# Matmuls of a product ordered by width, a first pair of accumulators in other PSUM banks, and two small moves at a phase change

## The chip, the core and the metric

The kernel runs on one core of one Trainium2 chip. The metric is the device time of an execution in microseconds (us). Engines are named as in the profile: PE is TensorE (matmuls), DVE is VectorE, ACT is ScalarE, POOL is GpSimd, SP is SyncE, which here only issues transfers (DMAs).

## What is computed

One encoder layer on 512 tokens of width 2048 in float32, and a last RMS norm. With `conv` a depthwise convolution over the tokens, and `attend` a neighbourhood attention on an 8 x 64 grid of tokens with 16 heads of 64:

```python
xn = rms_norm(x, attn_norm_g)
u_val, u_gate, q, k, v = split(xn @ w_in)            # 2048 -> 5 x 1024
a = silu(layer_norm(conv(u_val * sigmoid(u_gate), 31 taps)))
b = attend(q, k, v, rpb)
x = x + concat(rms_norm(a), rms_norm(b)) @ w_out     # 2048 -> 2048
up = conv(rms_norm(x) @ w_up, 3 taps)                # 2048 -> 2 x 5632
gate, val = split(up)
x = x + (silu(gate) * val) @ w_down                  # 5632 -> 2048
out = rms_norm(x, final_norm_g)
```

## The kernel before, in words

**Precision.** Each float32 weight tile is loaded as `raw` (128 x 1024, 512 KB) and split into two tiles of a reduced format (float32r): ACT copies the high half `whi` (L125), and DVE subtracts it from the raw tile for the low half `wlo` (L126). The other operands are split in the same way. A full product takes three matmuls: high by high, low by high, high by low (`mm3`, L138, L141, L142).

**Weights.** `plan` is a list of all weight units in order of use. `weights()` hands out the next one and makes the loads and splits of the units up to three further on (AHEAD = 3). Four tiles of `whi` and of `wlo` exist (NW = 4), and nine of `raw`.

**Order.** The tile framework's scheduler orders each engine's queue by priorities, which follow the program text; `shifted(by)` changes them for a block, and `pin` keeps an instruction in program order. Side work (statistics, factors, residual loads) is written as generators: `steps` is a list of them, and `tick(m)`, called behind a matmul, runs one more step of the first one, with its instructions issued after that matmul. PSUM has eight banks: three under the tag "mm", two under "sc" (one tile of two banks), two under "tr" and one under "po".

**Stages.** (times of the profiled execution)

1. To about 505 us: projection and attention. `first_glu` (L337) does the first two output tiles together, in two "mm" banks; then `project` (L315 on) does one tile of 48 matmuls after the other, each in an "mm" bank. `gated` (L350 on) takes a pair of tiles: DVE multiplies the gate tile by `rstd` (L352), ACT takes the sigmoid (L353), DVE multiplies twice more (L354, L356, the latter reads the second tile and writes `ch`), and 31 steps of the convolution follow on DVE (L363, L367). `stats1` computes `rstd`, which needs a square root on ACT (L225), two matmuls of `ones` (`st`, L237) and a copy (L239). Ahead of all that, a tiny activation (L109) runs on ACT, with the function Copy.
2. To about 703 us: the output projection.
3. 703 to 1578 us, the up stage. For each of 44 f's, `up` (L685 on) computes two tiles (gate and value) by seven products of half the size (a Strassen-Winograd scheme; products in the order TURN = 3, 2, 4, 5, 1, 0, 6). In six of the products the operand is one tile of 512 columns, high half and low half beside each other (256 each): for each of 8 blocks of the weight one matmul of the high weight by all 512 columns (L694), and one of the low weight by the 256 high columns (L697), in turn. Product 2 uses `mm3` with 256 columns. Accumulators `pa`, `pd_`, `pb`, `pe`, `pc_` are copied between products: ACT copies `pa` into `pd_` (L704) before product 4 may add to `pa`. Sums of weights are made on DVE (L653, L655) and by accumulating DMAs. Afterwards `hidden` multiplies by a norm factor (L748, L749), convolves (`conv3`: ACT L737, DVE L738, L739) and multiplies gate and value; results go to DRAM.
4. From 1578 us: the down stage. Seven products again (TURN2 = 3, 0, 4, 1, 2, 6, 5), each of 22 units of weight; a unit has 12 matmuls of 512 columns on four accumulators (L819, L820, L821). The left operands `ho` are made by `operand` (ACT L776 for the high half, DVE L777 for the low one) from the hidden tiles, which are read back from DRAM except for the last four. `again` makes operands ahead, into the list `pre`, while the last f runs: one operand, of hidden tiles that are not written to DRAM. `four` gives the accumulators: for products 3, 4, 2 and 5 two in the "sc" banks, where `pa` lay, and two in the "tr" banks; for products 0, 1 and 6 three "mm" banks and the "po" bank. `factors3` (L850 on) loads four tiles of the final norm's weights (`g3`) and multiplies two of them by -1 (L855); it is put into `steps` ahead of product 3. `taken` and `ready` add residual and accumulators; `write` normalises and stores at the end.

Of the kernel before, what the change touches and what calls it, by code (L numbers as in the profile page):

```python
# [10 lines left out]
F32 = mybir.dt.float32  # L11
F32R = mybir.dt.float32r
AF = mybir.ActivationFunctionType
ALU = mybir.AluOpType
AX = mybir.AxisListType

P = 128
D = 2048
S = 512
# [15 lines left out]
U = 8  # L35
# [5 lines left out]
H = S // 2  # L41
NK = NF // 2
KEEP = 4
# [10 lines left out]
TURN2 = (3, 0, 4, 1, 2, 6, 5)  # L54
Q = D // 2 // S
# [17 lines left out]
def layer(ctx: ExitStack, tc: tile.TileContext, xT, xn, w_in, w_out, w_up, w_down, par, tab, g3, out):  # L73
    nc = tc.nc
# [5 lines left out]
    psm = ctx.enter_context(tc.tile_pool(name="psm", bufs=3, space=bass.MemoryType.PSUM))  # L80
    psa = ctx.enter_context(tc.tile_pool(name="psa", bufs=1, space=bass.MemoryType.PSUM))
# [9 lines left out]
    def t2(name, dt=F32):  # L91
        return tp.tile([P, S], dt, tag="t2k", name=name)
# [13 lines left out]
    ones = consts.tile([P, P], F32, name="ones")  # L106
    nc.vector.memset(ones, 1.0)
    idle = t2("idle")
    nc.scalar.activation(idle[:, :1], ones[:, :1], AF.Copy)  # L109
    ps = psm.tile([P, S], F32, tag="mm", name="warm")  # L110
    for _ in range(WARM):
        nc.tensor.matmul(ps[:, :P], ones, ones, start=True, stop=True)
# [5 lines left out]
    def raw_unit(src, n):  # L118
        raw = t4([P, U * P], "raw")
        return raw, nc.sync.dma_start(raw[:, :n], src)  # L120

    def parts(raw, n):
        hi = wpool.tile([P, U * P], F32R, tag="whi", name="whi", bufs=NW)
        lo = wpool.tile([P, U * P], F32R, tag="wlo", name="wlo", bufs=NW)
        i = nc.scalar.activation(hi[:, :n], raw[:, :n], AF.Copy)  # L125
        j = nc.vector.tensor_sub(lo[:, :n], raw[:, :n], hi[:, :n].bitcast(F32))  # L126
        return hi, lo, i, j
# [5 lines left out]
    tight = []  # L133
# [11 lines left out]
    steps, asteps = [], []  # L145
# [105 lines left out]
    pin = tc.keep_in_program_order  # L251
# [24 lines left out]
    for j, n in enumerate((NC_, 0)):  # L276
        raw, i = raw_unit(w_in[n, :, U * P:2 * U * P], U * P)
        pin(i)
        w = parts(raw, U * P)
# [9 lines left out]
    for step in ORDER:  # L289
        i = next(a_ if step == "a" else q_)  # L290
# [44 lines left out]
        late.append(lambda: gated(i, pg, pv))  # L335

    def first_glu():  # L337
        two = [psm.tile([P, S], F32, tag="mm", name="pj") for _ in range(2)]
        for u in range(KD // U):
            ws = weights(), weights()  # L340
            for k in range(U):
                kk = u * U + k
                for ps, w in zip(two, ws):
                    hi, lo, at = w[k]
                    m = mm3(ps, (hi, lo), at, xs[kk][0], xs[kk][1], kk == 0, kk == KD - 1)
            for _ in range(2):
                tick(m)
        late.append(lambda: gated(0, *two))
# [180 lines left out]
    p, n = -1, 0  # L529
# [51 lines left out]
    comb = [[] for _ in range(7)]  # L581
# [85 lines left out]
    order2 = [*range(NK - KEEP // 2, NK), *range(NK - KEEP // 2)]  # L667
# [17 lines left out]
    def up(f, done):  # L685

        def product(c, ps, more):
            hi, lo = wt = weights()
            for k in range(U):
                m, w = comb[c][k], slice(k * P, (k + 1) * P)  # L690
                if c == 2:
                    i = mm3(ps[:, :H], wt, k, m[:, :H], m[:, H:], k == 0, k == U - 1)
                    continue
                i = nc.tensor.matmul(ps, hi[:, w], m, start=k == 0 and not more, stop=False, skip_group_check=more)  # L694
                if k == 0 and tight:
                    pin(i)
                i = nc.tensor.matmul(ps[:, :H], lo[:, w], m[:, :H], start=False, stop=k == U - 1,  # L697
                                     skip_group_check=more)
            tick(i)
            done(TURN.index(c), i)  # L700

        def copied(to, ps):
            with shifted(-100):
                nc.scalar.activation(to, ps, AF.Copy)  # L704

        def folded(to, ps):
            nc.scalar.activation(to, ps[..., H:], AF.Copy)
            add(to, to, ps[..., :H])

        product(3, pa, False)  # L710
        tight[:] = [1] * (f > 0)
        copied(pd_, pa)
        product(2, pc_, False)
        w = t2("w")[:, :H]
        nc.scalar.activation(w, pc_[:, :H], AF.Copy)
        product(4, pa, True)
        copied(pe, pa)
        product(5, pd_, True)
        g = t2("g")
        folded(g[:, :H], pd_)  # L720
        product(1, pa, True)
        copied(pb, pa)
        product(0, pe, True)
        v = t2("vl")
        by = v.rearrange("p (i t) -> p i t", i=2)
        folded(by[:, 1], pa)
        folded(by[:, 0], pe)
        add(by, by, w.unsqueeze(1).broadcast_to([P, 2, H]))
        product(6, pb, True)
        folded(g[:, H:], pb)  # L730
        return g, v
# [26 lines left out]
    def operand(c, k):  # L758

        if c in (3, 5, 6):  # L760
            src = hs[2 * k + (c != 3)][:, H if c == 6 else 0:][:, :H]
        else:
            (b11, b12), (b21, b22) = ((hs[i][:, :H], hs[i][:, H:]) for i in (2 * k, 2 * k + 1))
            t = t2("hc")
            src, m = t[:, :H], t[:, H:]
            if c == 2:
                nc.vector.tensor_sub(src, b22, b12)
            elif c == 1:
                nc.vector.tensor_sub(src, b11, b12)
            else:  # L770
                nc.vector.tensor_sub(m, b11, b12)
                nc.vector.scalar_tensor_tensor(src, b22, -1.0, m, op0=ALU.mult, op1=ALU.subtract)
                if c == 0:
                    nc.vector.scalar_tensor_tensor(src, src, -1.0, b21, op0=ALU.mult, op1=ALU.subtract)
        t = t2("ho", F32R)
        nc.scalar.activation(t[:, :H], src, AF.Copy)  # L776
        nc.vector.tensor_sub(t[:, H:], src, t[:, :H].bitcast(F32))  # L777
        return t
# [3 lines left out]
    pre = []  # L782

    def again(at, i):
        if at == 1:
            pre.extend(operand(TURN2[0], k) for k in order2[:KEEP // 2 - 1])
        for _ in range(6):
            if back:
                f = back.pop(0)
                hs[f] = t2("h")  # L790
                behind(nc.gpsimd.dma_start(hs[f], hd[f]), i)
# [56 lines left out]
    gs = []  # L848

    def factors3():  # L850
        for d in range(2 * Q):
            g = t2("g3")
            nc.sync.dma_start(g, g3[:, d * S:(d + 1) * S])
            if d >= Q:
                nc.vector.tensor_scalar(g, g, -1.0, None, op0=ALU.mult)  # L855
            gs.append(g)
            yield

    sq = [sm.tile([P, 2, 2 * Q], F32, tag="sq", name="sq") for _ in range(2)]
# [1 line left out]
    def taken(x, ps):  # L861

        for a, b in zip(x, ps):
            add(a, a, b)
            yield
# [36 lines left out]
    def run(c, ps, more):  # L902
        for _ in product2(c, ps, more):
            pass
# [3 lines left out]
            yield from x  # L908

    a = four(True)  # L910
    steps.append(factors3())
    run(3, a, False)
    e3 = rest(0, 0)
    steps.append(taken(e3, a))
    b = four(False)
    run(0, b, False)
    e0 = rest(0, 1)
    steps.append(taken(e0, b))
    run(4, a, True)
    e4 = rest(1, 0)  # L920
    steps.append(taken(e4, a))
    b = four(False)
# [78 lines left out]
```

## Time and profile before

| | us |
|---|---|
| median of 3 runs | 2015.14 (2013.87 to 2018.29) |
| the profiled execution's own time | 2016.07 |
| its span in the trace | 2014.3 |
| mean granted clock of PE | 0.997 |
| PE busy | 1994.4 |
| DVE busy | 1599.6 |
| ACT busy | 1105.2 |

A row of the timeline has start and duration in us, engine, line of the kernel, operation, tiles (written <- read), shape and count, and in brackets the idle time before it with the instruction or transfer that ended it. Matmuls overlap in the rows, since the next one starts before the one ahead has left the array; the distance between starts is the time that one costs. In the table of windows a row has the stretch, its length, and the busy time of each engine with its count of instructions, then the clock that PE was granted (1.00 is full), the share of the DMA engines' time, and GB/s.

### The profile page before, as it was taken

What the parts mean: (1) busy time and instruction counts of PE and PEld (TensorE: products, weight loads), DVE (VectorE), ACT (ScalarE), POOL (GpSimd) and SP (SyncE); (2) the same over time, 40 slices, a digit from 0 to 9 for tenths busy, and PEclk for the clock granted to TensorE, in tenths of its full rate; (3) what the DMA queues carried; (4) which work ended last, traced back from release to release, by engine and by line L of the source; (5) the groups of instructions that cost most, each with busy time, mean ns of one, the idle gap of its engine ahead of it and who ended that gap; (6) DMA issues with size and microseconds to landing.
All of it is one profiled execution on the core that took longest, in us unless ns stands there. A gap on an engine that the chain in (4) does not pass through costs nothing.

```text
span 2014.3 us, 28373 instructions
## 1 busy us (share of the span) xinstructions
PE 1994.4 (99%) x10525; PEld 1685.5 (84%) x10525; DVE 1599.6 (79%) x2296; ACT 1105.2 (55%) x1729; POOL 226.1 (11%) x310
## 2 busy tenths in 40 slices
PE   9999999999999999999999999999999999999998
PEld 7878888877788888888888888888888788888886
DVE  5994798498547888888888888888888798886765
ACT  7234423448525676666666666666666645554654
POOL 0110111110001111111111111111110400000000
PEclk9999999999999999999999999999999999999999
DMA  9677767776858879998999999999986976666563
GB/s 341 167 218 181 177 170 202 183 182 199 256 147 220 203 206 263 244 267 235 265 240 258 253 253 251 251 256 248 258 239 170 375 229 212 218 212 195 191 210 114
DMA packets 143114, 451.01 MB, mean 224 GB/s; under 512 B 15232, under 2 KB 23936, under 8 KB 141568
## 3 DMA queue, kind: packets, MB, share of 16 engines
q1 hardware_dynamic: 90608, 293.98, 43.6%
q0 software_dynamic: 42624, 148.92, 34.2%
q10 hardware_dynamic: 9744, 6.30, 1.0%
q8 instruction: 82, 1.34, 0.3%
q14 instruction: 56, 0.46, 0.1%
HBM read 430.27 MB, written 111.15 MB: 269 GB/s over the span
## 4 chain that ended last, share of the span: by engine, by line
PE 94%; DMA 2%; DVE 2%; ACT 1%; issue 0%; SPq 0%; DVEq 0%; ACTq 0%
PE pu L694 25%; PE pu L697 12%; PE pd L821 7%; PE pd L819 7%; PE pd L820 7%; PE pj L138 6%; PE pj L141 6%; PE pj L142 6%; PE po L138 3%; PE po L141 3%; PE po L142 3%; PE pu L141 2%; PE pu L138 2%; PE pu L142 2%; DVE y L367 1%; DMA xn<-in_xn 1%
## 5 line engine op out<-in xcount | busy, mean ns | idle before, releaser
L125 ACT ACTIVATE whi<-raw 128x1024 fp32r<-128x1024 f32 x572 | 605.5, 1059 | 722.4 <-PE pj L141 211.7
L126 DVE TENSOR_TENSOR wlo<-raw,whi 128x1024 fp32r<-128x1024 f32 x572 | 699.0, 1223 | 304.1 <-ACT whi L125 274.9
L694 PE MATMUL pu<-xc,whi 128*128 128x512 f32 x2112 | 748.2, 399 | 0.0
L697 PE MATMUL pu<-xc,wlo 128*128 128x256 f32 x2112 | 593.1, 281 | 0.0
L694 PEld LDWEIGHTS pu<-xc,whi 128*128 128x128 f32 x2112 | 396.8, 188 | 96.9 <-issue 0.2
L697 PEld LDWEIGHTS pu<-xc,wlo 128*128 128x128 f32 x2112 | 399.0, 189 | 0.3 <-issue 0.2
L138 PE MATMUL pj<-xh,whi 128*128 128x512 f32 x624 | 246.8, 398 | 1.4 <-DVE gate L352 1.4
L142 PE MATMUL pj<-xh,wlo 128*128 128x512 f32 x624 | 243.7, 390 | 0.8 <-DVE wlo L126 0.8
L141 PE MATMUL pj<-xl,whi 128*128 128x512 f32 x624 | 244.4, 392 | 0.1
L821 PE MATMUL pd<-whi,ho 128*128 128x512 f32 x616 | 240.1, 391 | 4.0 <-DVE ho L777 4.0
L819 PE MATMUL pd<-whi,ho 128*128 128x512 f32 x616 | 240.5, 391 | 0.5 <-ACT ho L776 0.5
L820 PE MATMUL pd<-wlo,ho 128*128 128x512 f32 x616 | 240.4, 390 | 0.0
L367 DVE SCALAR_TENSOR_TENSOR y<-ch,prm,y 128x507 f32<-128x507 f32 (+14 forms) x240 | 169.9, 742 | 3.2
L194 POOL DMA_DIRECT2D ws<-in_w_down x88 | 79.4, 902 | 568.1 <-DMA ws<-ws 279.0
L138 PEld LDWEIGHTS pj<-xh,whi 128*128 128x128 f32 x624 | 117.5, 188 | 30.2 <-issue 3.5
L821 PEld LDWEIGHTS pd<-whi,ho 128*128 128x128 f32 x616 | 116.0, 188 | 29.3 <-DVE ho L777 5.3
L142 PEld LDWEIGHTS pj<-xh,wlo 128*128 128x128 f32 x624 | 117.5, 188 | 26.1 <-DVE wlo L126 1.3
L141 PEld LDWEIGHTS pj<-xl,whi 128*128 128x128 f32 x624 | 117.7, 189 | 24.0 <-DVE xl L257 0.5
L819 PEld LDWEIGHTS pd<-whi,ho 128*128 128x128 f32 x616 | 115.9, 188 | 25.1 <-ACT ho L776 0.9
L820 PEld LDWEIGHTS pd<-wlo,ho 128*128 128x128 f32 x616 | 116.1, 188 | 24.6 <-DVE wlo L126 0.3
L643 POOL DMA_DIRECT2D raw<-in_w_up x88 | 85.2, 968 | 344.6 <-DMA raw<-in_w_up 85.6
L138 PE MATMUL pu<-xc,whi 128*128 128x256 f32 x352 | 99.7, 283 | 0.5 <-ACT xc L586 0.5
(185 smaller groups left out, 2524.4 us busy)
## 6 DMA issues: line engine op xcount, KB each, us to landing
raw<-in_w_up SPq DMA_DIRECT2D x220, 512.0 KB, 8.0
ws<-in_w_down POOLq DMA_DIRECT2D x132, 512.0 KB, 7.7
raw<-in_w_up POOLq DMA_DIRECT2D x88, 512.0 KB, 9.8
raw<-ws SPq DMA_DIRECT2D x88, 512.0 KB, 4.3
raw<-in_w_in SPq DMA_DIRECT2D x78, 512.0 KB, 5.1
raw<-in_w_down SPq DMA_DIRECT2D x66, 512.0 KB, 4.2
ws<-ws POOLq DMA_DIRECT2D x44, 512.0 KB, 7.9
raw<-in_w_out SPq DMA_DIRECT2D x32, 512.0 KB, 5.1
```

What stands on the lines that cost most here:

```text
L125: i = nc.scalar.activation(hi[:, :n], raw[:, :n], AF.Copy)
L126: j = nc.vector.tensor_sub(lo[:, :n], raw[:, :n], hi[:, :n].bitcast(F32))
L138: i = nc.tensor.matmul(ps, hi[:, a], mh, start=start, stop=False, skip_group_check=more)
L141: nc.tensor.matmul(ps, hi[:, a], ml, start=False, stop=False, skip_group_check=more)
L142: return nc.tensor.matmul(ps, lo[:, a], mh, start=False, stop=stop, skip_group_check=more)
L367: nc.vector.scalar_tensor_tensor(y[:, a:b], h[:, a + j - PAD:b + j - PAD], prm[:, o + j:o + j + 1], y[:, a:b], op0=ALU.mult, op1=ALU.add)
L643: nc.gpsimd.dma_start(a[c], w_up[f, q2], accum_op=ALU.add)
L694: i = nc.tensor.matmul(ps, hi[:, w], m, start=k == 0 and not more, stop=False, skip_group_check=more)
L697: i = nc.tensor.matmul(ps[:, :H], lo[:, w], m[:, :H], start=False, stop=k == U - 1, skip_group_check=more)
L819: nc.tensor.matmul(ps[i], h[:, t], wh[:, d], start=start and not more, stop=False, skip_group_check=more)
L820: nc.tensor.matmul(ps[i], h[:, t], wl[:, d], start=False, stop=False, skip_group_check=more)
L821: return nc.tensor.matmul(ps[i], h[:, tl], wh[:, d], start=False, stop=stop, skip_group_check=more)
```

## The change

Four edits. In six of the seven products of an f, the eight matmuls with high weights and 512 columns come first, then the eight with low weights and 256 columns. The tiny first activation is a square root, and the two tiles of `first_glu` lie in the "tr" banks. `factors3` issues its four loads one per step and the two multiplications after all of them, and stands behind `taken(e0, b)`, which puts it into the third product (4) of the down stage. `again` makes two operands.

```diff
-    nc.scalar.activation(idle[:, :1], ones[:, :1], AF.Copy)
+    nc.scalar.activation(idle[:, :1], ones[:, :1], AF.Sqrt)
...
     def first_glu():
-        two = [psm.tile([P, S], F32, tag="mm", name="pj") for _ in range(2)]
+        two = [psa.tile([P, S], F32, tag="tr", name="pj", bufs=2) for _ in range(2)]
...
         def product(c, ps, more):
             hi, lo = wt = weights()
-            for k in range(U):
-                m, w = comb[c][k], slice(k * P, (k + 1) * P)
-                if c == 2:
+            if c == 2:
+                for k in range(U):
+                    m = comb[c][k]
                     i = mm3(ps[:, :H], wt, k, m[:, :H], m[:, H:], k == 0, k == U - 1)
-                    continue
-                i = nc.tensor.matmul(ps, hi[:, w], m, start=k == 0 and not more, stop=False, skip_group_check=more)
-                if k == 0 and tight:
-                    pin(i)
-                i = nc.tensor.matmul(ps[:, :H], lo[:, w], m[:, :H], start=False, stop=k == U - 1,
-                                     skip_group_check=more)
+            else:
+                for part, n in ((hi, S), (lo, H)):
+                    for k in range(U):
+                        i = nc.tensor.matmul(ps[:, :n], part[:, k * P:(k + 1) * P], comb[c][k][:, :n],
+                                             start=part is hi and k == 0 and not more,
+                                             stop=part is lo and k == U - 1, skip_group_check=more)
+                        if part is hi and k == 0 and tight:
+                            pin(i)
             tick(i)
             done(TURN.index(c), i)
...
         if at == 1:
-            pre.extend(operand(TURN2[0], k) for k in order2[:KEEP // 2 - 1])
+            pre.extend(operand(TURN2[0], k) for k in order2[:KEEP // 2])
...
     def factors3():
         for d in range(2 * Q):
-            g = t2("g3")
-            nc.sync.dma_start(g, g3[:, d * S:(d + 1) * S])
-            if d >= Q:
-                nc.vector.tensor_scalar(g, g, -1.0, None, op0=ALU.mult)
-            gs.append(g)
+            gs.append(t2("g3"))
+            nc.sync.dma_start(gs[d], g3[:, d * S:(d + 1) * S])
+            yield
+        for g in gs[Q:]:
+            nc.vector.tensor_scalar(g, g, -1.0, None, op0=ALU.mult)
             yield
...
     a = four(True)
-    steps.append(factors3())
     run(3, a, False)
     e3 = rest(0, 0)
     steps.append(taken(e3, a))
     b = four(False)
     run(0, b, False)
     e0 = rest(0, 1)
-    steps.append(taken(e0, b))
+    steps += [taken(e0, b), factors3()]
     run(4, a, True)
```

## The prediction

> **What bounds the kernel now.** I read the page first, then the timeline of TensorE (PE) stage by stage.
>
> ```profile
> span 2014.3 us, 28373 instructions
> ...
> PE 1994.4 (99%) x10525; PEld 1685.5 (84%) x10525; DVE 1599.6 (79%) x2296; ACT 1105.2 (55%) x1729; POOL 226.1 (11%) x310
> ...
> PE 94%; DMA 2%; DVE 2%; ACT 1%; issue 0%; SPq 0%; DVEq 0%; ACTq 0%
> ...
> L694 PE MATMUL pu<-xc,whi 128*128 128x512 f32 x2112 | 748.2, 399 | 0.0
> ```
>
> PE is busy 99% of the span and carries 94% of the chain that ended last. So an edit pays in two ways only: PE issues its steps faster, or one of its few stalls goes. L694 has 2112 instructions with no idle time before them: the up stage waits for nothing, and its length is a sum of steps. Durations of single matmuls overlap, so I use distances between starts:
>
> ```profile
> 1204.51 0.28 PE L138 MATMUL pu<-xc,whi 128*128 128x256 f32 x1
> ...
> 1207.39 0.40 PE L694 MATMUL pu<-xc,whi 128*128 128x512 f32 x1
> 1207.63 0.28 PE L697 MATMUL pu<-xc,wlo 128*128 128x256 f32 x1
> ...
> 1215.86 0.40 PE L694 MATMUL pu<-xc,whi 128*128 128x512 f32 x1
> ...
> 1227.22 0.40 PE L694 MATMUL pu<-xc,whi 128*128 128x512 f32 x1
> ...
> 1699.70 0.39 PE L821 MATMUL pd<-whi,ho 128*128 128x512 f32 x1
> ...
> 1703.78 0.39 PE L821 MATMUL pd<-whi,ho 128*128 128x512 f32 x1
> ```
>
> From 1204.51 to 1207.39 lie the 24 matmuls of product 2, all 256 wide: 2.88/24 = **0.120 us** a step. From 1207.39 to 1215.86 lie three mixed products, 24 pairs of 512 and 256: 8.47/24 = **0.353 us** a pair. From 1699.70 to 1703.78 lie 18 steps of 512 only: 4.08/18 = **0.2267 us**. The two pure steps make 0.3467, so a mixed pair costs 0.006 us more than its halves. The row at 1207.63 shows where: 512 to 256 takes 0.24 instead of 0.2267.
>
> **Part 1, the sorted product.** In every f six of seven products change: 44 x 6 = 264 (x 8 = the 2112 of L694). Before, 8 pairs: 8 x 0.353 = 2.823. After, 7 steps from 512 to 512, 7 from 256 to 256, and one of each turn, which together are a pair's 0.353: 7 x 0.2267 + 7 x 0.120 + 0.353 = 2.780. Gain 0.0434 a product, 264 x 0.0434 = **-11.5 us**. Upper bound of the gain: all turns free, 8 x 0.006 x 264 = 13; lower bound: nothing, if a run of 512 in this stage doesn't go at the 0.2267 of the down stage. I take the rows' value, for they are the same instruction in the same shape.
>
> The Trainium skill, "TensorE: Matmul & The Clock Gate", section "Back-to-back issue gap", speaks against this part: its gap grows with the columns alone, with a fixed few cycles per instruction, so the order of widths would change nothing. By its figures an estimate is 216 + 109 = 325 ns a pair; the trace has 353, and 353 is more than its own parts, so the trace doesn't agree. By the page this part is 0, which is a rival below.
>
> Sorting also moves things. hi is released 8 x 0.120 = 0.96 us before the product's end instead of at its end, so ACT's split of the next weights (L125) comes earlier; lo isn't needed until 8 x 0.2267 = 1.8 us later, which relaxes DVE. What could break is the copy of pa to pd_ (L704), for which product 4 waits because it writes pa again:
>
> ```profile
> 1225.44 0.57 ACT L704 ACTIVATE pu<-pu 128x512 f32<-128x512 f32 x1
> 1226.07 0.82 ACT L737 ACTIVATE uy<-g,prm 128x512 f32<-128x512 f32 x1
> ```
>
> ```profile
> 1224.21 1.22 DVE L655 TENSOR_TENSOR raw<-raw 128x1024 f32<-128x1024 f32 x1
> 1225.35 0.68 DVE L748 TENSOR_TENSOR g<-g,rstd 128x512 f32<-128x512 f32 x1
> ```
>
> The copy ends at 1226.01, product 4 starts at 1227.22: slack 1.2 us. In the built order of the changed kernel ACT's first uy (L737 here) stands ahead of the copy, and it waits for DVE's g (L748). But there DVE does g before the sum of L655, not behind it, so g comes about 1.1 us earlier and uy's 0.8 fits ahead of the copy. I cost the rest of the period at 0; without that cover each us is paid 44 times (third rival). DVE and ACT have room:
>
> ```profile
> core 0: us, PE busy (x) PEld busy (x) DVE busy (x) ACT busy (x) POOL busy (x), PEclk, DMA share, GB/s
> 1200.00:1300.00 100.00, 100.00 (x607) 88.68 (x605) 86.07 (x107) 62.98 (x91) 16.14 (x20) 1.00 0.93 255
> 1597.00:1605.00 8.00, 5.37 (x17) 3.95 (x16) 3.79 (x7) 2.46 (x7) 3.48 (x7) 0.79 1.04 396
> ```
>
> The first f is different, because its operands arrive late:
>
> ```profile
> 709.05 0.38 PE L138 MATMUL pu<-xc,whi 128*128 128x256 f32 x1 [0.53 <-ACT xc L586]
> ```
>
> Before, lo matmuls fill the time until the last operand arrives near 709. After, the built order runs hi ones, part of product 2, waits longer, and has some 8 lo matmuls (0.96) and the copy (0.57) still ahead of product 4: **+1.5 us** (0 to 2).
>
> **Part 2, the first pair in other banks, and the Sqrt table.** The head of the kernel:
>
> ```profile
> 41.17 0.39 PE L142 MATMUL pj<-xh,wlo 128*128 128x512 f32 x1
> 42.19 1.13 PE L237 MATMUL st<-dg,ones 128*128 128x512 f32 x2 [0.63 <-DVE dg L234]
> 44.73 0.79 PE L138 MATMUL pj<-xh,whi 128*128 128x512 f32 x1 [1.41 <-DVE gate L352]
> ...
> 47.88 0.43 PE L141 MATMUL pj<-xl,whi 128*128 128x512 f32 x1
> ...
> 57.22 0.39 PE L138 MATMUL pj<-xh,whi 128*128 128x512 f32 x1
> ...
> 102.20 0.50 PE L142 MATMUL pj<-xh,wlo 128*128 128x512 f32 x1 [0.85 <-DVE wlo L126]
> ```
>
> The fourth projection product (48 matmuls) waits for the bank of the first pair until 44.73, and then its first 7 steps take 0.45 instead of 0.2267, until 47.88 (3.15 instead of 1.59): a slowed clock after idling. After, it needs no wait and the pair of st matmuls stands behind 18 of its steps: start 41.40, 48 x 0.2267 = 10.88, st at most 1.13 and about 0.9: end 53.2, **4.0 us earlier** than 57.22. This would be the whole gain, if the next product had its weights. DVE decides:
>
> ```profile
> 47.86 0.54 DVE L363 TENSOR_SCALAR y<-ch,prm 128x512 f32<-128x512 f32 x1
> 48.43 0.74 DVE L367 SCALAR_TENSOR_TENSOR y<-ch,prm,y 128x497 f32<-128x497 f32 x1
> ...
> 52.66 1.22 DVE L126 TENSOR_TENSOR wlo<-raw,whi 128x1024 fp32r<-128x1024 f32 x1
> ...
> 57.42 0.69 DVE L356 TENSOR_TENSOR ch<-pj,gate 128x512 f32<-128x512 f32 x1 [0.62 <-PE pj L142]
> ...
> 100.93 2.36 DVE L126 TENSOR_TENSOR wlo<-raw,whi 128x1024 fp32r<-128x1024 f32 x2
> 103.20 0.69 DVE L423 TENSOR_TENSOR k<-pj,rstd 128x512 f32<-128x512 f32 x1
> ```
>
> Before, DVE splits the next product's lo at 52.66, ahead of ch (L356), which waits until the fourth product has ended (57.42). In the built order after, ch stands ahead of that split, with three operations between. So lo now comes at a fixed time behind the fourth product's end: 0.2 (57.22 to 57.42) + 0.6 (ch) + 0.66 + 0.57 + 0.66 (L367, L363, L367) + 1.22 = 3.9, while PE wants it at its third step, 0.45 after. (On DVE a start follows about 0.08 before the busy time of the one ahead ends: L363, 0.54, is followed after 0.57, but L367's 0.74 I take as 0.66 and ch's 0.69 as 0.6.) PE waits about 3.5 us, gives back 3.5 of the 4.0, and pays the slowed clock again: about +1.6, as at 44.73. Sum here +1.1. The same turn comes once more near 102: k (L423), which waits for its product's end, and three L367 stand ahead of the split that before was done at 100.93 ahead of k. Wait 0.2 + 0.6 + 3 x 0.66 + 1.22 - 0.45 = 3.5 instead of the 0.85 at 102.20, and a slowed clock of 1.6, less some slower steps there: +4.1. Later splits are early in both orders. Sum +5.2, with the moves between **+5.4 us** (2 to 7; without the two waits it would be -4).
>
> The Sqrt edit takes the table load out of the chain ahead of st:
>
> ```profile
> 38.65 1.28 ACT L225 ACT_TABLE_LOAD   x1
> ```
>
> After, st isn't waited for by PE at once, so these 1.28 us only move the gates earlier: 0, included above.
>
> **Parts 3 and 4, the phase change.**
>
> ```profile
> 1578.40 0.40 PE L819 MATMUL pd<-whi,ho 128*128 128x512 f32 x1
> ...
> 1582.58 0.51 PE L821 MATMUL pd<-whi,ho 128*128 128x512 f32 x1 [1.41 <-DVE ho L777]
> ...
> 1600.72 0.58 PE L821 MATMUL pd<-whi,ho 128*128 128x512 f32 x1 [2.63 <-DVE ho L777]
> ...
> 1604.47 0.39 PE L821 MATMUL pd<-whi,ho 128*128 128x512 f32 x1
> ```
>
> ```profile
> 1582.44 0.75 DVE L708 TENSOR_TENSOR vl<-vl,pu 128x256 f32<-128x256 f32 x2
> ...
> 1599.90 0.43 DVE L855 TENSOR_SCALAR g<-g 128x512 f32<-128x512 f32 x1 [5.87 <-DMA g<-in_g]
> 1600.25 0.42 DVE L777 TENSOR_TENSOR ho<-h,ho 128x256 fp32r<-128x256 f32 x1
> ```
>
> By the built order the row at 1582.58 is the 9th step of the stage and the one at 1604.47 its 84th. At 0.2267 the 83 steps between the first and the last row take 18.8; they took 26.07. So **7.25 us** are lost here. At 1582.58 PE waits for the low half of the second operand: 8 x 0.2267 = 1.8 after 1578.40 it would have been due, it came after 4.18, so 2.4 went (a wait on ACT's high half just before among them). From 1600.72 to 1604.47 nine steps took 3.75 instead of 2.04, so 1.7 is slowed clock (0.79 in the window from 1597 above), and 2.63 the wait before it: PE waits for an operand (1600.25) that stands in DVE's queue behind the -1 multiplication of a weight of the final norm, which waited 5.87 for its DMA. That is 4.3; the remaining 0.5 are slower steps.
>
> After, both operands are ready and the first multiplication comes two units later with its load already back. What is late next at the first place: two of the four accumulators lie in pa's banks, which DVE must first fold (L708 at 1582.44, done 4.8 after the start). PE wants them after the 12 steps that the first two units do in the other banks (2.7). In the built order one low half (0.42) goes from ahead of the fold, and the last split ahead of it gets its hi 0.96 earlier (part 1): 4.8 - 0.4 - 1.0 = 3.4, a wait of 0.7 (0 to 2). The second stall goes; the four g3 loads move on SP from here
>
> ```profile
> 1587.95 1.81 SPq L853 DMA_DIRECT2D g<-in_g  x4
> ```
>
> to behind single weight loads, one per unit, during the third product, where a load is issued three units (3 x 12 x 0.2267 = 8.2 us) ahead. They take 0.45 us of queue each: hidden; without that cover some 1.8 us. The xr loads come one place earlier: 0. Of the loads some may still be late (396 GB/s, DMA share 1.04 in that window), for which I keep 0.25: 7.25 - 0.7 - 0.25 = **-6.3 us** (-7.3 to -3).
>
> **Sum.** -11.5 + 1.5 + 5.4 - 6.3 = **-10.9 us**. The profiled execution took 2016.07 (its span 2014.3 and 1.8 around it), 0.9 over the median of the runs; 2016.07 - 10.9 = 2005.2, and on the median 2015.14 - 10.9 = **2004.2 us**.
>
> **Rivals.**
> R1, the splits of lo don't hold PE up in the head, because DVE gets through that stretch sooner than I worked out. For: at 52.66 the split lay 3.8 us ahead of the latest start that PE would allow (57.22 + 0.45 - 1.22), and only an order is built, no times. Against: ch can't run before its product ends, and the split is behind it. Then part 2 is -4 and not +5.4: 2004.2 - 9.4 = **1994.8**.
> R2, sorting gives nothing: steps of 512 in the up stage cost more than in the down stage, and the sum of a product stays. Against: the measured steps. 2004.2 + 11.5 = **2015.7**.
> R3, slower: the copy of L704 behind uy becomes the last to arrive, and product 4 waits in each of 44 f's. Against: the slack of 1.2. It decides from a copy 1.2 us later than now; it eats the gain at 10.9/44 = 0.25 us of wait per f, and at 0.5 us it costs 22: 2004.2 + 22 = **2026.2**.
>
> **How the numbers follow.** Forecast 0.72, R1 0.10, R2 0.10, R3 0.08. The forecast's own range by its bounds is 1998 to 2010.5. To leave no more than 0.18 out I reach down to R1 and leave R2 and R3: **1994 to 2011**. Within 0.2% (4 us, about what a measurement of this kernel can tell from no change) lies R2. Faster 0.82, same 0.10, slower 0.08.
>
> **What would show it.** In the changed profile: a mixed product from its first hi to the next product in 2.78 us; L704 ending a us ahead of product 4; PE starting the fourth projection product near 41.4, then waits of some 3.5 us on wlo near 53 to 57 and 102 to 106, each followed by slow steps; no wait on ho near 1582 and 1600, and a short one on the fold. The prediction is wrong if a product takes 2.82, if PE shows waits in every f, or if the lo splits of the head come in time.

## The result and the profile after

The changed kernel takes 2010.44 us (median of 15 runs, 2008.65 to 2015.02) against 2014.44 us (15 runs, 2012.79 to 2018.29): ratio 0.9977, 95% interval 0.9969 to 0.9985. That is 3.0 to 6.2 us faster, where 10.9 was forecast. A second set of runs gave 0.9963 (0.9949 to 0.9977), about 7.5 us. The execution that was profiled took 2008.65, the shortest of the 15, and the one of before 2016.07, longer than its median; their difference, 7.4, is thus more than that of the medians. The experiments come back to this.

The page of the changed kernel, where L696 stands for both kinds of matmuls of the sorted product:

```profile
span 2006.9 us, 28334 instructions
...
PE 96%; DVE 2%; ACT 1%; DMA 1%; issue 0%; SPq 0%; DVEq 0%; ACTq 0%
...
L696 PE MATMUL pu<-xc,whi 128*128 128x512 f32 x2112 | 529.8, 392 | 0.2 <-ACT pu L706 0.2
...
L142 PE MATMUL pj<-xh,wlo 128*128 128x512 f32 x624 | 244.7, 392 | 7.1 <-DVE wlo L126 7.1
L138 PE MATMUL pj<-xh,whi 128*128 128x512 f32 x624 | 247.5, 399 | 0.0
...
L821 PE MATMUL pd<-whi,ho 128*128 128x512 f32 x616 | 239.7, 389 | 0.5 <-DVE vl L710 0.5
```

The three places that the prediction worked on show at once. L138 no longer waits for a gate and the phase change has 0.5 us of waiting left instead of 4.5, but L142 now waits 7.1 us for `wlo` in the head. The long idle times are therefore exchanged rather than gone. By stages (start of the up stage, start of the down stage, last matmul of the down stage):

| us | before | after | difference | forecast |
|---|---|---|---|---|
| up stage starts | 702.16 | 707.63 | +5.5 | +5.4 |
| up stage | 876.24 | 869.61 | -6.6 | -10.0 (-11.5 + 1.5) |
| down stage, matmuls | 426.35 | 419.80 | -6.5 | -6.3 |
| from the start of the last matmul to the end | 9.54 | 9.85 | +0.3 | 0 |

So one term of four is off by 3.4 us: the up stage. Here is its step, in the timeline of PE in the changed kernel (neighbouring matmuls of one kind are one row, with their count):

```profile
1209.75 2.00 PE L696 MATMUL pu<-xc,whi 128*128 128x512 f32 x8
1211.59 1.12 PE L696 MATMUL pu<-xc,wlo 128*128 128x256 f32 x8
1212.55 2.00 PE L696 MATMUL pu<-xc,whi 128*128 128x512 f32 x8
1214.38 1.12 PE L696 MATMUL pu<-xc,wlo 128*128 128x256 f32 x8
```

The eight steps of 256 from 1211.59 to 1212.55 take 0.96, or 0.120 each as forecast. The eight of 512 (1209.75 to 1211.59) take 1.84, not 8 x 0.2267 = 1.81. Averaged over 35 f's, the distances from one start to the next within a product are (ns):

```
512 columns: 233.3 235.8 228.3 232.5 230.8 226.7 226.7 226.7
256 columns: 113.3 119.1 120.0 120.0 120.0 120.0 120.0 120.0
sum 2793
```

The first five steps of 512 behind a stretch of 256 are slower, 27 ns together; the first two of 256 behind 512 are quicker, 8 ns together. A turn there and back costs 0.020 us and not the 0.006 that it costs in alternating pairs. A product takes 2.793 instead of 2.780; the forecast gain of 0.0434 a product is 0.031, and 264 x 0.031 = 8.2 instead of 11.5.

The head in the changed kernel: the timeline of DVE, of ACT and of PE, and then two windows behind PE's waits (columns: stretch, length, busy time of each engine with its instructions, granted clock of PE, DMA share, GB/s):

```profile
47.18 0.69 DVE L352 TENSOR_TENSOR gate<-pj,rstd 128x512 f32<-128x512 f32 x1 [4.84 <-ACT rstd L239]
...
52.89 0.73 DVE L367 SCALAR_TENSOR_TENSOR y<-ch,prm,y 128x498 f32<-128x498 f32 x1
53.53 0.68 DVE L356 TENSOR_TENSOR ch<-pj,gate 128x512 f32<-128x512 f32 x1
...
55.89 2.35 DVE L126 TENSOR_TENSOR wlo<-raw,whi 128x1024 fp32r<-128x1024 f32 x2
```

```profile
46.54 0.60 ACT L239 ACTIVATE rstd<-st 128x512 f32<-128x512 f32 x1 [6.38 <-PE st L237]
...
51.17 0.64 ACT L353 ACTIVATE gate<-gate 128x512 f32<-128x512 f32 x1 [2.08 <-DVE gate L352]
51.71 1.99 ACT L125 ACTIVATE whi<-raw 128x1024 fp32r<-128x1024 f32 x2
```

```profile
45.49 1.02 PE L237 MATMUL st<-dg,ones 128*128 128x512 f32 x2
...
57.16 0.50 PE L142 MATMUL pj<-xh,wlo 128*128 128x512 f32 x1 [3.35 <-DVE wlo L126]
...
106.38 0.80 PE L142 MATMUL pj<-xh,wlo 128*128 128x512 f32 x1 [3.78 <-DVE wlo L126]
```

```profile
core 0: us, PE busy (x) PEld busy (x) DVE busy (x) ACT busy (x) POOL busy (x), PEclk, DMA share, GB/s
58.40:61.80 3.40, 3.40 (x9) 2.63 (x8) 3.40 (x5) 0.00 (x0) 0.00 (x0) 0.50 0.60 180
107.00:109.50 2.50, 2.50 (x7) 1.96 (x6) 2.50 (x4) 0.00 (x0) 0.00 (x0) 0.50 0.76 223
```

The two waits are there with nearly the size that was forecast (3.35 and 3.78 for 3.5), each followed by steps of 0.427 at a granted clock of 0.50. But the first three fences tell another story than the forecast. `st` runs at 45.49 (42.19 before), so rstd, the first gate multiplication, the second sigmoid and the split of `wlo` that PE waits for (55.89, before 52.66) all come 3.2 us later. `ch`, which was to hold up that split, waited for nothing: its row has no idle time, it began right behind the operation ahead of it. It was close, though: PE began the next product at 53.19, only 0.3 us ahead of `ch`.

The phase change, timeline of PE in the changed kernel:

```profile
1577.24 0.40 PE L821 MATMUL pd<-whi,ho 128*128 128x512 f32 x1
...
1580.63 0.50 PE L821 MATMUL pd<-whi,ho 128*128 128x512 f32 x1 [0.48 <-DVE vl L710]
```

One wait is left, on the fold, as forecast: the thirteenth step comes 3.39 us after the first instead of 12 x 0.2267 = 2.72, so 0.67 late (0.7 forecast).

### The profile page after: what moved, and what is told of

Its sections match the earlier page's. It is cut to its first block, busy times and chain, and to the rows that moved or that the text cites. A ratio compares the mean times of both kernels' runs of the same rounds, so it can differ in the third digit from the quotient of the medians.

```text
span 2006.9 us, 28334 instructions
## 1 busy us (share of the span) xinstructions
PE 1985.5 (99%) x10525; PEld 1688.0 (84%) x10525; DVE 1598.5 (80%) x2296; ACT 1095.9 (55%) x1728; POOL 225.8 (11%) x310
## 4 chain that ended last, share of the span: by engine, by line
PE 96%; DVE 2%; ACT 1%; DMA 1%; issue 0%; SPq 0%; DVEq 0%; ACTq 0%
PE pu L696 37%; PE pd L821 7%; PE pd L822 7%; PE pd L823 7%; PE pj L138 7%; PE pj L141 7%; PE pj L142 7%; PE po L138 3%; PE po L141 3%; PE po L142 3%; PE pu L141 2%; PE pu L142 2%; PE pu L138 2%; DVE y L367 1%; PE po L495 1%; PE sc L453 1%
## 5 line engine op out<-in xcount | busy, mean ns | idle before, releaser
L696 PE MATMUL pu<-xc,whi 128*128 128x512 f32 x2112 | 529.8, 392 | 0.2 <-ACT pu L706 0.2
L696 PEld LDWEIGHTS pu<-xc,whi 128*128 128x128 f32 x2112 | 379.9, 189 | 68.8 <-issue 0.5
L696 PEld LDWEIGHTS pu<-xc,wlo 128*128 128x128 f32 x2112 | 288.1, 190 | 20.5
L696 PE MATMUL pu<-xc,wlo 128*128 128x256 f32 x2112 | 294.5, 282 | 0.0
L142 PE MATMUL pj<-xh,wlo 128*128 128x512 f32 x624 | 244.7, 392 | 7.1 <-DVE wlo L126 7.1
L138 PE MATMUL pj<-xh,whi 128*128 128x512 f32 x624 | 247.5, 399 | 0.0
L367 DVE SCALAR_TENSOR_TENSOR y<-ch,prm,y 128x509 f32<-128x509 f32 (+14 forms) x240 | 170.0, 740 | 3.2
L142 PEld LDWEIGHTS pj<-xh,wlo 128*128 128x128 f32 x624 | 118.0, 189 | 33.0 <-DVE wlo L126 8.0
L138 PEld LDWEIGHTS pj<-xh,whi 128*128 128x128 f32 x624 | 118.0, 189 | 28.4 <-issue 3.7
L138 PE MATMUL pu<-xc,whi 128*128 128x256 f32 x352 | 99.8, 284 | 1.4 <-ACT xc L586 1.4
```

What stands on the lines that cost most here:

```text
L138: i = nc.tensor.matmul(ps, hi[:, a], mh, start=start, stop=False, skip_group_check=more)
L142: return nc.tensor.matmul(ps, lo[:, a], mh, start=False, stop=stop, skip_group_check=more)
L367: nc.vector.scalar_tensor_tensor(y[:, a:b], h[:, a + j - PAD:b + j - PAD], prm[:, o + j:o + j + 1], y[:, a:b], op0=ALU.mult, op1=ALU.add)
L696: i = nc.tensor.matmul(ps[:, :n], part[:, k * P:(k + 1) * P], comb[c][k][:, :n], start=part is hi and k == 0 and not more, stop=part is lo ...
```

## Experiments

Theory A at first: the terms are the kernel's own, the head's waits come from the places of `ch` and `k` in DVE's queue, and a turn of widths has a fixed price. Rivals: the head's waits have another cause, and the profiled execution was not typical.

### Without the head edits, and with the splits first on DVE

The first run is the changed kernel once more, the second leaves out the bank move and the Sqrt, the third adds order edges (no semaphores) that put `ch` of the second pair and the first `k` behind the splits of the next product:

```diff
+        los.append(j)                      # in parts(), j is the subtraction that makes wlo
...
-        nc.vector.tensor_mul(h, pv, g)
+        j = nc.vector.tensor_mul(h, pv, g)
+        if i == 1:
+            tc.add_manual_dep(j.ins, los[-3].ins.name, NoSync, reason="behind lo")   # likewise for k, p == 0
```

NoSync stands for the dependency's class, which orders two instructions of one engine's queue and adds nothing else.

> The changed kernel once more, to see which stages differ from profile to profile. Theory A (the terms of the first profile are the kernel's own): head +5.5 us against before (the up stage starts at 707.6 instead of 702.2), up stage 869.6 instead of 876.2, down stage 419.8 instead of 426.3; time 5 to 8 us below before. Theory B (that profile was a lucky one): one of the stages, most likely the down stage with its late loads, is 2 to 4 us longer this time, and the time is 4 to 5 us below before.

> Sorted products and both edits at the phase change, without the bank move and the Sqrt. Theory A (the head costs 5.5 us by its two waits on wlo): the up stage starts near 702.2 as before, and the time is about 5.5 us below the changed kernel, 10 to 13 below before. Rival (the lateness of the head is made up later by transfers that then arrive in time): the up stage starts earlier, but the time is within 2 us of the changed kernel.

> The changed kernel with an order edge on DVE: the second pair's ch and the first k stand behind the splits of lo that the next product needs, as in the kernel before. Theory A (order on DVE makes both waits, the bank move itself gains 4): no wait of 3.5 us near 53 and 102, the up stage starts about 4 us earlier than before (near 698), the time 9.5 us below the changed kernel and 14 to 17 below before. Rival (the splits can't be ready any earlier, because raw tiles or hi come late): waits of 1 to 4 us on whi or wlo remain there, and the up stage starts at 702 or later.

Measured: the changed kernel 2009.59, without the head edits **2003.25** (ratio to before 0.9930, 0.9916 to 0.9944), with the splits first 2007.41 (0.9950, 0.9936 to 0.9965). The head edits cost 6.3 us: theory A holds for the amount (13.9 below before by the medians, 10 to 13 expected). The up and down stages were the same to 0.1 us in the first two runs (869.61 and 419.86), so those terms are the kernel's own.

For the cause, theory A fell at the first wait. With the splits ahead of `ch`, as in the kernel before, PE and DVE read:

```profile
57.85 0.50 PE L145 MATMUL pj<-xh,wlo 128*128 128x512 f32 x1 [3.33 <-DVE wlo L128]
...
105.57 0.50 PE L145 MATMUL pj<-xh,wlo 128*128 128x512 f32 x1 [2.29 <-DVE wlo L128]
```

```profile
47.90 0.69 DVE L355 TENSOR_TENSOR gate<-pj,rstd 128x512 f32<-128x512 f32 x1 [3.63 <-ACT rstd L242]
```

The first wait is as long as without the edges, and the up stage started at 707.96. The distance from the first gate multiplication to the end of the first wait is 9.95 us here and 9.98 in the changed kernel: what comes late is the start of the chain, rstd. The second wait fell from 3.78 to 2.29, with three DVE operations fewer ahead of its split, so about 1.5 us of that one does come from the place of `k`.

### st first

Theory C: the bank move lets the scheduler put the pair of `st` matmuls behind 18 steps of the fourth product, since PE no longer has to wait there; rstd, the gates and all that DVE does behind them start later. From the first gate multiplication to the second wait DVE is busy nearly all the time, in the changed kernel (a row of the windows):

```profile
47.18:106.38 59.20, 52.07 (x222) 42.22 (x221) 56.27 (x81) 15.34 (x16) 7.24 (x10) 0.97 0.62 153
```

56.27 of 59.20 us (in the window of before, 43.98 to 102.20, it is 54.78 of 58.22). So PE's second wait should end a fixed time behind that multiplication. Four runs: an order edge that puts `st` ahead of the fourth product; the same with the edges on DVE and with alternating order of high and low weights (below); only the Sqrt; and the changed kernel without the bank move, with the alternating order.

```diff
+        sts.append(nc.tensor.matmul(ps, ones, dg, start=True, stop=True))     # st, in root_steps
...
+        if edge:                           # first matmul of project(1)
+            tc.add_manual_dep(i.ins, sts[0].ins.name, NoSync, reason="behind st")
```

> The changed kernel with an order edge on PE: the pair of st matmuls (for rstd) stands ahead of the fourth projection product, as in the kernel before, instead of behind 18 of its steps. New theory C: from the first gate multiplication on, DVE is busy for 55 to 56 of some 58 us, so it bounds this stretch, and PE's second wait on wlo ends 57 to 59 us after that multiplication, whatever PE did before. The multiplication then starts near 43.2 instead of 47.2, the wait near 53 goes, the one near 100 ends at about 101.8 instead of 106.3, and the up stage starts 4 to 6 us earlier than in the changed kernel; time 4 to 6 us below it, no gain of 4 against the head of before. Rival A (the order of the splits behind ch and k makes the waits): the wait near 53 stays or the up stage starts within 1 us of the changed kernel's.

> As the run with st first, with the order edges that put ch and k behind the splits of lo, and with the alternating order of high and low weights. Theory C: the second wait on wlo ends near 100, 1.5 to 2 us earlier than with st alone, since four operations more stand behind it; period 19.58; time 8 to 12 us below the changed kernel. Rival (the longer wait of PE near 97 slows the clock each time): a part of it, about 2 us, goes to slow steps.

> Only the Sqrt of part 2 on the kernel before. Theory C: st starts about 0.8 earlier (41.4, when PE has done the product ahead of it, instead of 42.2), the first gate multiplication and with it the second wait come 0.8 earlier, time 0.8 us below before, plus or minus the slow steps behind a stall. Rival (the table load is hidden, as the prediction had it: 0): the first gate multiplication stays at 44.0.

> The changed kernel without the bank move, with the alternating order of high and low weights. Theory C: head as before less 0.8 (up stage starts at 699.8 to 701.4), period 19.58, down stage 419.8 to 420.8; time 17 to 19 us below before, 2.5 to 4 below the run without the head edits. Rival: the extra stall that the alternating order had at the phase change (0.9) eats most of it.

Measured: `st` first 2004.83 (0.9946, 0.9933 to 0.9958), 4.8 below the changed kernel's 2009.59 of the other set (by the ratios to before only 3.4, with intervals that just overlap); with all edges 2003.86 (0.9939, 0.9927 to 0.9952); only the Sqrt 2013.79 (0.9987, 0.9978 to 0.9996); without the bank move and alternating **1999.71** (0.9924, 0.9910 to 0.9937). With `st` first, DVE and PE:

```profile
44.89 0.69 DVE L356 TENSOR_TENSOR gate<-pj,rstd 128x512 f32<-128x512 f32 x1 [2.17 <-ACT rstd L243]
```

```profile
102.91 0.50 PE L146 MATMUL pj<-xh,wlo 128*128 128x512 f32 x1 [3.79 <-DVE wlo L126]
```

The wait near 53 is gone, PE arrives at 99.0 for the second one and stands there 3.8 us. What the bank move gives PE is taken back by DVE at the next place where they meet: the up stage started at 704.29, still 2.1 later than in before. One thing is not separated. With `st` first, `ch` also lies behind the split without any edge for it:

```profile
53.57 1.22 DVE L126 TENSOR_TENSOR wlo<-raw,whi 128x1024 fp32r<-128x1024 f32 x1
...
57.63 0.68 DVE L360 TENSOR_TENSOR ch<-pj,gate 128x512 f32<-128x512 f32 x1
```

A late rstd is enough for the first wait (the run with the splits first). Whether the place of `ch` alone would also have made it is not shown, since no run has an early rstd with `ch` ahead of the split.

The distance from the first gate multiplication to the end of the second wait is 58.0 us here, 58.0 with all edges (42.56 to 100.59), 59.2 in the changed kernel, 57.7 with the splits first, and 58.2, 56.7 and 56.7 in the kernel before, without the head edits and with the Sqrt alone: near 57 to 59 whether PE comes early or not. In the last three PE waits only 0.85, so there the two engines are about level, and these three alone would not show it. One run falls outside: in the changed kernel with the alternating order (below) the distance is 60.3 (46.20 to 106.51). There 12 steps ran slowed behind the first wait (2.4 us, in the changed kernel 1.6), and DVE stood longer for a high half, for which ACT had waited for a matmul; DVE, then ACT:

```profile
65.10 1.23 DVE L126 TENSOR_TENSOR wlo<-raw,whi 128x1024 fp32r<-128x1024 f32 x1 [2.31 <-ACT whi L125]
```

```profile
64.00 1.06 ACT L125 ACTIVATE whi<-raw 128x1024 fp32r<-128x1024 f32 x1 [9.38 <-PE pj L141]
```

In the changed kernel that wait of DVE is 1.21. So theory C holds with a reserve: DVE's 56.3 us of work set most of the distance, and slowed steps of PE can add to it.

Several expectations missed. With `st` first the first gate multiplication came at 44.89 and not near 43.2; seven steps (1.4 us) had run slowed from 15.4 on. The edges on DVE did not shorten the distance (58.0 again), and the run with all edges was not 8 us below the changed kernel: 12 steps followed its wait at the lowered clock (2.4 us), and a new wait came up in the output projection. The waits of PE in that run (total us, times, longest):

```profile
PE pj L149 <- DVE wlo L128: 3.8, 1, 3.8
PE trx L609 <- DVE x L618: 2.5, 1, 2.5
```

The run without the bank move and alternating is 16.6 below before (17 to 19 expected), and by its ratio it cannot be told from the run without the head edits (0.9930, 0.9916 to 0.9944). The Sqrt alone gained 2.6 us by the medians (0.8 to 4.4). Its profiled execution has the first gate multiplication at 44.20, not earlier than before, since the chain ahead of it started later in that execution. Measured from the chain's start (the sum of L310 on DVE) the gain shows: to the first gate multiplication it is 5.32 us in all six profiles without the bank move and the Sqrt, and 4.44 in both with the Sqrt and without the bank move. So the Sqrt takes 0.9 out of the chain, as theory C had it, and 0.9 lies within the interval of the gain. The prediction had it at 0.

The bank move alone, one execution:

> Only the bank move of part 2 on the kernel before. Theory C (the bank move lets the scheduler put st behind 18 steps of the next product, which delays rstd): first gate multiplication near 47.2 as in the changed kernel, a wait of 3 to 4 near 53, the second wait ends 57 to 60 us after the first gate multiplication, the up stage starts 4 to 7 us later than before. Rival (without the Sqrt the order differs and st stays early): first gate multiplication near 44.

2020.50 against 2015.91 in the same set. The first gate multiplication came at 47.45, the second wait ended at 106.66 (59.2 behind it), the up stage started at 708.04, 5.9 later than before. So the bank move alone carries the head's loss, in this one execution, and the Sqrt isn't part of it.

### The price of a turn

In one run three of the six products do the low weights first, so that 512 follows 256 three times in an f instead of six; in another a product has four high, four low, four high, four low.

```diff
-                for part, n in ((hi, S), (lo, H)):
+                for part, n in ((lo, H), (hi, S)) if c in (4, 1, 6) else ((hi, S), (lo, H)):
...
-                for part, n in ((hi, S), (lo, H)):
-                    for k in range(U):
+                for part, n, k0 in ((hi, S, 0), (lo, H, 0), (hi, S, U // 2), (lo, H, U // 2)):
+                    for k in range(k0, k0 + U // 2):
```

> The changed kernel, but products 4, 1 and 6 do the low weights first, so that 512 columns follow 256 three times in an f instead of six. Theory A (each such turn costs 0.020 us over the next five steps): the period of an f falls from 19.64 to 19.58, 2.6 us in all. Rival (the extra 0.020 belongs to the start of each product, to new weights or another accumulator, not to the turn of widths): the period stays at 19.64. Third case: lo is now wanted first and DVE is late with it, so that PE waits on wlo, and the period is over 19.64.

> The changed kernel with four high, four low, four high, four low matmuls in a product, so twice as many turns of widths. Theory A (a turn to 512 after 256 costs 0.016 to 0.020 over the next steps): a product takes 2.774 + 2 x 0.016 to 0.020, the period of an f is 19.71 to 19.76, between sorted (19.64) and alternating (19.827). Rival (the extra 0.020 belongs to the start of a product): 19.64.

The start of product 2 in two f's next to each other, first of the alternating order, then of the groups of four:

```profile
1186.05 0.28 PE L138 MATMUL pu<-xc,whi 128*128 128x256 f32 x1
...
1205.62 0.28 PE L138 MATMUL pu<-xc,whi 128*128 128x256 f32 x1
```

```profile
1189.46 0.28 PE L138 MATMUL pu<-xc,whi 128*128 128x256 f32 x1
...
1209.18 0.28 PE L138 MATMUL pu<-xc,whi 128*128 128x256 f32 x1
```

The periods are 19.57 and 19.72 (medians over the f's 19.580 and 19.720), both as theory A had them; the start of a product costs nothing of its own. With 2.880 for product 2, a mixed product takes 2.774 plus 0.050 with eight turns (before), 0.033 with two, 0.020 with one. A turn costs 0.006, 0.017 and 0.020: more, the longer the stretches are that it joins. Why the five steps behind a stretch of 256 are slower stays open.

The alternating order took 2008.79 (0.9961, 0.9948 to 0.9975), not distinguishable from the changed kernel's 2009.59 in that set (the groups of four 2012.64 in one execution): 2.6 us are gained in the up stage, and 0.9 given back in the down stage (420.75), whose first fold now waits 1.4 instead of 0.5.

### The two edits at the phase change, one at a time

> Only the second ready operand on the kernel before. By the prediction's terms the stall at the start of the down stage shrinks from 2.4 to 0.7 us and the one 22 us later stays, 4.3 with its slow steps: down stage 426.4 - 1.7 = 424.6. Rival: the second stall moves with the order and changes too.

> Only the later loads of the final norm's weights on the kernel before. By the prediction's terms the second stall goes with its slow steps, the first stays: down stage 426.4 - 4.5 to 4.9 = 421.5 to 421.9. Rival: the operand there is late by its own transfer, and a wait of 1 us or more stays.

One execution each: 2008.44 and 2018.36 (2015.91 for before in that set). The matmuls of the down stage took 420.63 with the second operand alone, 423.17 with the later loads alone, 419.80 with both, 426.35 before. The split that the prediction gave is wrong: the second operand alone takes 5.7 of the 6.5, not 1.7. In that run the loads and the first multiplication stand where they stood in the program, and still PE doesn't wait for the operand behind that multiplication (it waits 1.28 for the fold). SP, then DVE, with the second operand alone:

```profile
1579.35 1.81 SPq L853 DMA_DIRECT2D g<-in_g  x4
```

```profile
1592.54 0.43 DVE L855 TENSOR_SCALAR g<-g 128x512 f32<-128x512 f32 x1 [3.09 <-DMA g<-in_g]
```

SP issued the loads 2.9 us behind the stage's start instead of 9.6 (1587.95 - 1578.40), because a weight load that in before went out ahead of them, 9.1 us behind the start, stands behind them here. DVE still waited 3.09 for their data, but began the multiplication 16.0 us behind the stage's start instead of 21.5, early enough for PE. With the later loads alone, the second stall went too, the first stayed, and 7 steps at the lowered clock (1.4 us) followed it. That execution is slower than before as a whole for reasons ahead of this stage: its up stage started at 707.29, after 8 slowed steps near 46 and a wait of 2.75 on `x` in the output projection. The edits overlap: either one removes the second stall, and the later loads add 0.8 to the second operand.

### Executions of the same kernel

> The kernel before, profiled once more. Theory D (what differs between executions of one kernel is how many steps run at the slowed clock behind its stalls, and the first microseconds; all else is the same to 0.1 us): up stage 876.2, down stage 426.4 less 1.6 where no slow steps follow its second stall, head without the slow steps behind the stall near 44 (then the up stage starts near 700.6 and not 702.2). Rival: the stages differ from execution to execution by transfers.

> As the run ahead, the same kernel. Theory D: slow steps behind none, one or two of the stalls, each worth 1.2 to 2.6 us, and no other difference over 0.5 us behind the first 40 us.

> The changed kernel, profiled once more. Theory D: up stage 869.6, down stage 419.8 to 419.9; behind each of its two waits of 3.8 on wlo 6 to 13 slow steps (1.2 to 2.6), so that the up stage starts at 707.6 to 710.

> As the run ahead, the same kernel. Theory D: the same stages, and slow steps behind both waits on wlo every time, since both are over 3.6 us long, where the 1.9 us stall of before is followed by slow steps in some executions only.

Times 2015.46 and 2015.21 for before, 2009.77 and 2010.32 for the changed kernel. Counting the steps of over 0.38 us between starts in every profile gives the stretches at the lowered clock (start in us: steps, us lost):

```
before   first profile  45.3: 6, 1.2    1601.1: 8, 1.6
before   second         1582.9: 7, 1.4
before   third          1600.5: 7, 1.4
changed  first profile  58.4: 8, 1.6    107.0: 6, 1.2
changed  second         58.1: 7, 1.4    107.0: 13, 2.6
changed  third          57.6: 7, 1.4    106.8: 11, 2.2
changed  fourth         58.1: 6, 1.2    107.1: 11, 2.2
```

Theory D holds for the larger part. The up and down stages are the same to 0.4 us in all these profiles (0.1 had been expected); what differs is the number of slowed steps, and by up to 0.9 us the first 44 us (first gate multiplication at 43.98, 44.87 and 44.51 before; 47.07 to 47.48 after). The first profile of before had the most slowed steps of its three, the first of the changed kernel the fewest of its four. By the means of the profiles the up stage starts at 701.7 before and 708.5 after: the head's loss is **6.8**, not 5.5. With -6.6 in the up stage, -6.4 in the down stage and +0.4 behind it the sum is -5.8, between the two sets of medians (-4.6 and -7.5 by their ratios).

## Why the prediction was wrong

- **What bounds the kernel** held: PE is on the chain for 96%, and nearly every us gained or lost is a step or a wait of PE.
- **Part 1, the sorted product**: the step that failed is "one of each turn, which together are a pair's 0.353". The price of a turn was taken from pairs that follow each other, where no stretch of one width occurs. In sorted products a turn costs 0.020, three times as much, and 264 of them take 3.3 us of the gain. The rows could not show it: in before no stretch of 512 follows a stretch of 256. The only place with such a turn is behind product 2, in whose rows the next product starts at 1207.39 with pairs. The measured gain of 8.2 lies inside the bounds of this part (13 and nothing), but the lower one was reasoned from slower steps of 512 in the whole stage; that a turn between long stretches may be dearer than one between pairs was not considered.
- The Trainium skill ("TensorE: Matmul & The Clock Gate", section "Back-to-back issue gap") gives a gap that depends on the columns alone, and calls it the gap of an isolated matmul. For a stream, as the prediction used it, it does not hold: the same sixteen matmuls take 2.824, 2.807 and 2.793 us in three orders. R2, by which sorting gives nothing, did not come about as a whole. Its reason was right in part: five of the eight steps of 512 do cost more than 0.2267.
- The first f cost 1.6 (27.88 instead of 26.51 from the stage's start to the second product 2, in a period otherwise 0.19 shorter), 1.5 forecast.
- The copy ahead of product 4 (R3) stayed in time: PE waited 0.2 us for it in the whole stage.
- **Part 2**: the amount held in the profile (+5.5 for +5.4), the cause didn't. I let `ch`, waiting for its product, hold up the split. The step that failed is that `st`, 18 steps back, "isn't waited for by PE at once" and so costs nothing. The runs show that it delays rstd by 3.2 us, and that DVE's 55 to 56 us of work behind it make PE's second wait end 57 to 59 us later. That the sum agreed is luck: DVE, late by rstd, came to `ch` at 53.53, 0.3 us behind the product's end, where the forecast had it at 0.2 behind. Of the order that the forecast blamed the second wait shows about 1.5 us; its share in the first wait is not separated. The two slowed stretches were taken at 1.6 each, and cost 1.2 to 2.6.
- The Sqrt was put at 0 by the same step; it takes 0.9 out of the chain to rstd.
- R1 named the same place, but with `st` first its gain of 4 didn't come: DVE is the bound there. That the early arrival of PE is worth nothing as long as DVE is full was not seen, though the rows of DVE ahead of 100.93 had hardly a gap.
- **Parts 3 and 4**: sum right (-6.3 forecast, -6.4 measured), the wait left on the fold too; the shares of the two edits wrong, since a stall with two causes was booked to one.
- **The median**: the sum of -10.9 was taken from a profile with more slowed steps (2.8 us) than the other two of before (1.4 each).
- **The range**: 1998 to 2010.5 is not what the parts' own bounds add up to; those reach from 1996.8 to 2021. So the 2010.44 that was measured lies inside the stated 1994 to 2011 without bearing out the sum.

Against the -5.8 of the means the forecast missed 5.1 us: 3.4 in the up stage (3.3 by the price of the turn), 1.4 in the head, 0.4 behind the last matmul, less 0.1 at the phase change. The 1.4 are slowed steps for the most part: in the head they cost 3.5 us on the average of the changed kernel (2.8 in its first profile) and 0.4 on that of before (1.2 in its first).

## What to carry to other kernels

A price taken from an alternating pattern doesn't hold for long stretches: ask where the trace shows the new neighbourhood, and where it doesn't, give the price a bound on both sides. When an edit takes away a wait, look what else stood in that gap: here two small matmuls slipped 18 steps back because PE was no longer idle, and the engine that waited for their result, not the edited one, set the time. Find the engine that is full up to the next meeting point before counting a gain ahead of it; without the two head edits the changed kernel is 6.3 us faster than with them, and the version with the lowest time (no bank move, the Sqrt, alternating widths) takes 0.9924 of the time of before (0.9910 to 0.9937).

## What was not expected of the hardware

- Behind a stretch of matmuls of 256 columns the first five of 512 take 233, 236, 228, 233 and 231 ns instead of 227, and the first two of 256 behind 512 take 113 and 119 instead of 120, the same in each of 35 periods.
- Behind each wait of 3.3 to 3.8 us on `wlo` in the profiles of the changed kernel 6 to 13 steps ran at a granted clock of 0.50 (0.427 us a step). Behind the stall of 1.41 near 44 of before they followed in two of the six profiles with that head, and in none of the two with the Sqrt and no bank move; so behind a stall of this length the loss (1.2 and 1.6 us there) comes in some executions and not in others. What decides it is not shown.
